# Sparse attention layer: the first eight heads' queries, values and keys made in steps of 512 columns instead of 256, in the order q, v, k

## The chip, the cores and the metric

The kernel runs on one core of one Trainium2 chip. Time is the device time of one execution in microseconds (us). The kernel before took 1060.66 us in the median of three runs (1060.22 to 1060.94). The five engines are TensorE (PE, matmuls; PEld are its weight loads), VectorE (DVE), ScalarE (ACT), GpSimd (POOL) and SyncE (SP), which here only issues DMAs. Each engine works through its own queue in order and waits on semaphores for the others.

## The reference

Four residual layers over a sequence of 512 tokens of width 1024: a gated short convolution, a sparse attention layer, a latent attention layer, and a second convolution. The change concerns the sparse attention layer alone:

```python
q, k, v, z, qi, ki, wi = jnp.split(xn @ w_in, cuts, axis=-1)
q = rope(rmsnorm(q.reshape(bsz, seq, B_HEADS, B_HEAD_DIM), q_norm), positions)
k = rope(rmsnorm(k.reshape(bsz, seq, B_HEADS, B_HEAD_DIM), k_norm), positions)
v = v.reshape(bsz, seq, B_HEADS, B_HEAD_DIM)
...
    rel = jax.nn.relu(jnp.einsum("qhd,sd->qhs", qi_b, ki_b).astype(jnp.float32))
    score = jnp.einsum("qh,qhs->qs", w_b.astype(jnp.float32), rel)
    score = jnp.where(chunk_visible(q_pos, k_pos), score, -jnp.inf)
    top_val, top_idx = lax.top_k(score, topk)
    logits = jnp.einsum("qhd,qkhd->qhk", q_b, k_sel).astype(jnp.float32) * scale
    p = jax.nn.softmax(logits, axis=-1).astype(v_sel.dtype)
    return jnp.einsum("qhk,qkhd->qhd", p, v_sel)
...
return (o * jax.nn.silu(z)) @ w_out
```

There are 16 heads of 64. An indexer of 8 small heads scores all keys for each query, the best 128 are kept, and attention runs over these. The kernel turns the choice into an additive mask and attends densely.

## The kernel before

Activations lie with features on partitions (128) and the 512 tokens along the row. Every large product is made of three matmuls: both operands are split into a high part (`whi`, `xh`) and a low rest (`wlo`, `xl`), and `products` (L279 to L281) adds high by high, high by low and low by high. The weights come by DMA into `raw`; ACT makes `whi` (L155), POOL makes `wlo` (L157), in units of 128 x 512 elements, at most three ahead of PE.

The layer first makes the indexer's projections, then three kinds of work. *Gate steps* (`pz`) multiply 128 columns of z into one bank of 512 tokens. *Query, key and value steps* (`pq`, `pk`, `pv`, function `tokens`) hold tokens on partitions: the activations are the stationary operand and the weight columns stream, 256 at a time for a group of four heads; two blocks of 128 tokens share a bank. *Index scores* (`si`) feed the choice: sixteen rounds of MAX and MATCH_REPLACE on DVE (L801, L802) for each of three query blocks.

After a query or key step, `query_key` copies each bank (ACT, L827), squares it (ACT, L829), sums the squares per head (DVE, L830), rotates (POOL ropea L553, DVE ropeb L557, POOL L560), and works out the norms: sums times a token factor (POOL, L840), mean (L272), a power of -0.5 (L274). For keys POOL also multiplies the tile by the norm (L853). Then `to_features` transposes on PE (L570, tile `tr`), ACT copies out the high part (L573) and DVE subtracts for the low part (L574). Queries are transposed without their norm, which is applied to the scores.

Attention goes through eight pairs of heads. Each pair's scores (`s`, L288) are read by DVE with the mask (L640), made exponentials by ACT (L643), normalised by POOL and ACT (L658, L660), transposed (`pt`, L670) and multiplied with the values (`o`, L691). A `Filler` puts the steps of the later heads between.

In the program, the first eight heads were made as two groups: four gate steps, then q, k, v of heads 0 to 3, two gate steps, q, k, v of heads 4 to 7, all woven with the choice in a ratio of costs (96 to 50). The third and fourth groups are filler during attention. This program order isn't the order on the engines: at build, the framework orders every engine's queue anew by a model of its own (L1184), within what data and buffers allow. Of matter here: eight PSUM banks (tags pj 2, pt 2, o 1, tr 1 and a pair for scores), four `qk` tiles for raw queries and keys, four `whi` and four `wlo` tiles, five `rp` tiles.

Of the kernel before, what the change touches and what calls it, by code (L numbers as in the profile page):

```python
# [17 lines left out]
P = 128  # L18
# [3 lines left out]
NT = S // P  # L22
# [49 lines left out]
def encoder(ctx: ExitStack, tc: tile.TileContext, a, out, depth=4):  # L72
# [20 lines left out]
    def tiny(name, n, dtype=F32, tag="tiny"):  # L93
        return sb.tile([P, n], dtype, name=name, tag=tag, bufs=24)
# [171 lines left out]
    minus_half = const([P, 16], "minus_half")  # L266
    pool.memset(minus_half, -0.5)

    def small_rsqrt(v, n, scale, out=None):

        m = tiny("mean", n)
        pool.tensor_scalar(m, v, scale, EPS, op0=OP.mult, op1=OP.add)  # L272
        y = tiny("y", n) if out is None else out
        pool.tensor_tensor(out=y, in0=m, in1=minus_half[:, :n], op=OP.pow)  # L274
        return y
# [460 lines left out]
    def layer_b(last):  # L736
# [82 lines left out]


        def query_key(group, which, scales, dst, banks):
            raw = []
            sums = tiny("hs", 16)

            def fin(i, b):
                x = tile_of("qk", "qk", (P, 2, 256))
                act_e.activation(x.rearrange("p t c -> p (t c)"), b, AF.Copy)  # L827
                q = tile_of("rp", "qk2", (P, 2, 256))
                act_e.activation(q.rearrange("p t c -> p (t c)"), b, AF.Square)  # L829
                dve.tensor_reduce(sums[:, 8 * i:8 * i + 8], q.rearrange("p t (h d) -> p (t h) d", d=64),  # L830
                                        axis=AX.X, op=OP.add)
                raw.append(x)
                x5, b5 = (y.rearrange("p t (h i j) -> p t h i j", h=4, i=2)
                          for y in (x, b.rearrange("p (t c) -> p t c", c=256)))
                C, T = (tab[:, 2 * i:2 * i + 2] for tab in (tq if which == "q" else tk))
                rotate(x5, x5, C, T, b5)

            yield from tokens(group, act, fin, banks)
            v = tiny("hv", 16)
            pool.tensor_tensor(out=by_head(v), in0=by_head(sums), in1=st["r2"][:, :, None].to_broadcast([P, NT, 4]),  # L840
                               op=OP.mult)
            y = small_rsqrt(v, 16, 1.0 / 64)
            if which == "q":
                pool.tensor_tensor(out=scales, in0=by_head(y), in1=st["rs"][:, :, None].to_broadcast([P, NT, 4]),
                                   op=OP.mult)
            else:
                f = tiny("hf", 16)
                pool.tensor_tensor(out=by_head(f), in0=by_head(y), in1=st["r"][:, :, None].to_broadcast([P, NT, 4]),
                                   op=OP.mult)
            for i, x in enumerate(raw):  # L850
                if which == "k":
                    x3 = x.rearrange("p t (h d) -> p (t h) d", d=64)
                    pool.tensor_tensor(out=x3, in0=x3, in1=f[:, 8 * i:8 * i + 8, None].to_broadcast([P, 8, 64]),  # L853
                                       op=OP.mult)

            for p in range(2):
                to_features(dst[p], lambda t: raw[t // 2][:, t % 2, p * P:(p + 1) * P], P)

        def values(group, dst, banks):
            def fin(i, b):  # L860
                for j in range(2):
                    t = 2 * i + j
                    act_e.activation(dst[i][:, j], b[:, j * 256:(j + 1) * 256], AF.Copy, scale=st["r"][:, t:t + 1])
# [4 lines left out]
        def project(g, tags):  # L868
            s = sets[g] = dict(qs=sb.tile([P, NT, 4], F32, name="qs", tag="qs", bufs=2))
            for n, w in enumerate("qkv"):  # L870
                banks = [bank("p" + w, tags[n % len(tags)]) for _ in range(2)]
                group = a["b_" + w][g]
                if w == "v":
                    s[w] = [tile_of("v", "v", (P, 2, 256)) for _ in range(2)]
                    yield from values(group, s["v"], banks)
                else:
                    s[w] = [[tile_of("T", w + "T", dtype=F32R) for _ in range(2)] for _ in range(2)]
                    yield from query_key(group, w, s["qs"], s[w], banks)

        def job(pair, after, fill):  # L880
            g, i = divmod(pair, 2)

            def scores(outs, t):
# [8 lines left out]
        gate = []  # L892
        token_factors()
# [7 lines left out]
        attention([job(p, p // 2 - 2, ends[p:p + 2]) for p in range(8)],  # L901
                  Filler([project(g, ["pj"]) for g in range(2, 4)] + [gate_steps(a["b_z"][6:], R, gate)]))
# [178 lines left out]
    for i in range(depth):  # L1081
# [3 lines left out]
        elif kind == 1:  # L1085
            enter(a["b_idx"] + a["b_z"][:4])
            for g in range(4):
                enter([a["b_" + w][g] for w in "qkv"])
                if g == 0:
                    enter(a["b_z"][4:6])  # L1090
# [32 lines left out]
def pack(inputs):  # L1123
# [33 lines left out]
    for n, c in (("q", 0), ("k", 1024), ("v", 2048)):  # L1157
        groups["b_" + n] = [put(f"b_{n}_{i}", w, slice(c + 256 * i, c + 256 * i + 256)) for i in range(4)]
# [39 lines left out]
```

## Time and profile before

| | us |
|---|---|
| median of three runs | 1060.66 |
| the profiled execution | 1060.87 |
| its span, first to last instruction | 1059.1 |
| PE busy | 1043.1 |
| POOL busy | 693.9 |
| DVE busy | 525.1 |
| ACT busy | 511.8 |
| first index scores `si` start | 275.5 |
| first query step `pq` starts | 281.4 |
| first attention scores `s` start | 372.0 |

Times in the trace are counted from the span's start. Rows of groups give line, engine, operation, tiles, shape, count, then busy time, mean nanoseconds of one, and the idle time before them. Rows of the timeline give start and length in us. Rows of stretches give, for a window, the busy time and the number of instructions of each engine, the granted PE clock, the DMA share and GB/s. Matmuls overlap in the array, so their rate is read from start to start. The granted clock was 1.000 on average.

### The profile page before, as it was taken

The page shows a single profiled execution, that of the slowest core. Times are in us where ns is not written, and L with a number is a line of the kernel's source. Part 1 is how long each engine was busy: PE and PEld are TensorE (multiplying, and loading weights), DVE is VectorE, ACT ScalarE, POOL GpSimd, SP SyncE. Part 2 cuts the span into 40 slices and gives each one's busy share as a digit, 9 for nine tenths or more (in the row PEclk, how much of TensorE's full clock was granted, in tenths as well). Part 3 has the DMA queues.
Part 4 walks back from the last instruction along what each step waited for, and adds up shares of the span by engine and source line. Part 5 has one row for each costly group of instructions (what it writes and reads, how often), then busy time and mean ns, then how long its engine had stood idle before and what let it go on. Part 6 is the DMA issues. An engine that isn't in the chain of part 4 may idle for free.

```text
span 1059.1 us, 16258 instructions
## 1 busy us (share of the span) xinstructions
PE 1043.1 (98%) x6040; PEld 877.1 (83%) x6040; DVE 525.1 (50%) x1064; ACT 511.8 (48%) x1090; POOL 693.9 (66%) x645
## 2 busy tenths in 40 slices
PE   8999999999999999999999999999999999999998
PEld 6888888899798999998888777687777888888886
DVE  7784333434598984343535234454442654443321
ACT  6243323433444457666745447876764533333231
POOL 6656555666369799686539689788743856555552
PEclk9999999999999999999999999999999999999999
DMA  6333333323222121111223221101211333333332
GB/s 210 103 113 87 97 99 100 90 66 116 80 80 80 61 100 41 61 56 45 58 58 102 75 72 50 41 23 61 61 55 46 100 100 100 100 100 100 100 100 79
DMA packets 27150, 86.43 MB, mean 82 GB/s; under 512 B 3392, under 2 KB 4160, under 8 KB 27072
## 3 DMA queue, kind: packets, MB, share of 16 engines
q1 hardware_dynamic: 26928, 85.36, 26.2%
q8 instruction: 47, 0.77, 0.3%
q14 instruction: 31, 0.25, 0.1%
q10 hardware_dynamic: 144, 0.05, 0.0%
HBM read 83.30 MB, written 2.10 MB: 81 GB/s over the span
## 4 chain that ended last, share of the span: by engine, by line
PE 93%; DVE 3%; ACT 2%; issue 1%; DMA 1%; POOL 0%; SPq 0%; DVEq 0%; ACTq 0%
PE pa L281 10%; PE pa L279 10%; PE pa L280 10%; PE po L279 6%; PE po L281 6%; PE po L280 5%; PE o L691 4%; PE pt L670 3%; PE s L1064 3%; PE pz L279 2%; PE pz L281 2%; PE pz L280 2%; PE s L288 2%; PE tr L570 2%; PE pq L279 2%; PE pk L280 2%
## 5 line engine op out<-in xcount | busy, mean ns | idle before, releaser
L157 POOL TENSOR_TENSOR wlo<-raw,whi 128x512 fp32r<-128x512 f32 (+4 forms) x324 | 410.3, 1274 | 259.2 <-ACT whi L155 248.4
L155 ACT ACTIVATE whi<-raw 128x512 fp32r<-128x512 f32 (+3 forms) x328 | 196.8, 604 | 328.4 <-PE pa L280 159.3
L280 PE MATMUL pa<-xl,whi 128*128 128x512 f32 x512 | 199.5, 390 | 1.0 <-DVE xl L358 1.0
L279 PE MATMUL pa<-xh,whi 128*128 128x512 f32 x512 | 198.5, 390 | 0.9 <-ACT xh L357 0.8
L281 PE MATMUL pa<-xh,wlo 128*128 128x512 f32 x512 | 197.5, 389 | 0.0
L280 PEld LDWEIGHTS pa<-xl,whi 128*128 128x128 f32 x512 | 96.1, 188 | 21.9 <-DVE xl L358 1.9
L279 PEld LDWEIGHTS pa<-xh,whi 128*128 128x128 f32 x512 | 96.0, 188 | 21.3 <-ACT xh L357 1.5
L281 PEld LDWEIGHTS pa<-xh,wlo 128*128 128x128 f32 x512 | 96.1, 188 | 19.9
L658 POOL TENSOR_SCALAR p<-p,rc 128x128 f32<-128x128 f32 (+1 forms) x64 | 69.9, 1099 | 46.2 <-DVE rc L653 41.1
L643 ACT ACTIVATE p<-p,mn 128x128 f32<-128x128 f32 (+3 forms) x128 | 71.0, 557 | 18.2 <-DVE mn L640 18.0
L465 DVE TENSOR_TENSOR cg<-pa,R 128x512 f32<-128x512 f32 x16 | 11.0, 690 | 122.1 <-PE pa L281 119.8
L640 DVE CUSTOM_DVE_ANT_0 p<-s,cmask,qs 128x128 f32<-128x128 f32 (+2 forms) x80 | 37.7, 506 | 39.4 <-PE s L1064 26.7
L279 PE MATMUL pz<-xh,whi 128*128 128x512 f32 x128 | 51.5, 402 | 0.5 <-ACT qk L997 0.5
L281 PE MATMUL pz<-xh,wlo 128*128 128x512 f32 x128 | 50.8, 398 | 0.0
L280 PE MATMUL pz<-xl,whi 128*128 128x512 f32 x128 | 50.4, 394 | 0.0
L280 PE MATMUL po<-xl,whi 128*128 128x512 f32 x128 | 50.1, 391 | 0.0
L675 ACT ACTIVATE p<-pt 128x384 f32<-128x384 f32 (+1 forms) x80 | 38.8, 510 | 23.0 <-PE pt L670 22.6
L280 PE MATMUL po<-glo,whi 128*128 128x512 f32 x128 | 49.8, 389 | 0.0
L279 PE MATMUL po<-xh,whi 128*128 128x512 f32 x128 | 49.5, 400 | 0.0
L279 PE MATMUL po<-ghi,whi 128*128 128x512 f32 x128 | 49.5, 389 | 0.0
L274 POOL TENSOR_TENSOR y<-mean,minus_half 128x16 f32<-128x16 f32 (+1 forms) x18 | 48.8, 2711 | 0.8
L670 PE MATMUL pt<-ident,p 128*128 128x128 f32 x320 | 47.9, 277 | 0.6 <-ACT p L675 0.6
(244 smaller groups left out, 2423.5 us busy)
## 6 DMA issues: line engine op xcount, KB each, us to landing
raw<-in_a_in SPq DMA_DIRECT2D x63, 512.0 KB, 3.9
raw<-in_a_out SPq DMA_DIRECT2D x16, 512.0 KB, 3.9
raw<-in_b_z SPq DMA_DIRECT2D x8, 512.0 KB, 3.5
raw<-in_b_q SPq DMA_DIRECT2D x8, 512.0 KB, 3.4
raw<-in_b_k SPq DMA_DIRECT2D x8, 512.0 KB, 3.5
raw<-in_b_v SPq DMA_DIRECT2D x8, 512.0 KB, 3.5
raw<-in_c_z SPq DMA_DIRECT2D x8, 512.0 KB, 3.5
raw<-in_b_out SPq DMA_DIRECT2D x8, 384.0 KB, 3.2
```

The lines of the kernel that those rows point to most:

```text
L155: act_e.activation(hi[:, :, :n], raw[:, j:j + m], AF.Copy)
L157: e.tensor_tensor(out=lo, in0=raw[:, j:j + m, :n - few], in1=hi[:, :, :n - few].bitcast(F32), op=OP.subtract)
L274: pool.tensor_tensor(out=y, in0=m, in1=minus_half[:, :n], op=OP.pow)
L279: nc.tensor.matmul(o, l[0], r[0], start=first, stop=False)
L280: nc.tensor.matmul(o, l[0], r[1], start=False, stop=False)
L281: nc.tensor.matmul(o, l[1], r[0], start=False, stop=last)
L640: dve.tensor_tensor_reduce(out=p[:, w], in0=banks[e][:, w], in1=j["masks"](t), scale=j["qs"](e, t), scalar=-GONE, op0=OP.add, op1=OP.min, ...
L643: act_e.activation(p[:, w], p[:, w], AF.Exp, bias=mn[e][:, i:i + 1], scale=-1.0, accum_out=sm[:, e * n + i:e * n + i + 1])
L658: pool.tensor_scalar(p[:, w], p[:, w], rc[:, i:i + 1], None, op0=OP.mult)
L670: pe.transpose(b[:, i:i + P], p[:, i:i + P], ident)
L675: act_e.activation(p[:, :n], b[:, :n], AF.Copy)
L691: pe.matmul(o[64 * e:64 * e + 64, t * P:(t + 1) * P], j["v"](e, kb), x[e][:, i:i + P], start=first, stop=t == 0)
```

## The change

Heads 0 to 7 are made as one group: the weight matrices of q, k and v are cut into one block of 512 columns and two of 256. A step of 512 columns takes four banks (pj, pj, pt, pt), one for each block of 128 tokens. The order is three gate steps, q, gate step 4, v, gate step 5, k, gate step 6; the latter three gate steps use bank o, and transposes from there on use bank tr alone. Four steps of the choice are issued before the weave. `query_key` and `values` take any width: the sums of squares lie in one tile of 32 columns, worked on in place, and the power runs once for eight heads. Each raw tile holds one block of 128 tokens by 512 columns, as large as before. Heads 8 to 15 keep their steps of 256 columns. Weights enter in the new order.

```diff
     def tiny(name, n, dtype=F32, tag="tiny"):
-        return sb.tile([P, n], dtype, name=name, tag=tag, bufs=24)
+        return sb.tile([P, n], dtype, name=name, tag=tag, bufs=20)
...
     def small_rsqrt(v, n, scale, out=None):
-        m = tiny("mean", n)
+        m = tiny("mean", n) if out is not v else v
...
         def query_key(group, which, scales, dst, banks):
+            heads = group.n // 64
+            per = NT // len(banks)
             raw = []
-            sums = tiny("hs", 16)
+            sums = sb.tile([P, NT * heads], F32, name="hs", tag=f"hs{heads}", bufs=2)
 
             def fin(i, b):
-                x = tile_of("qk", "qk", (P, 2, 256))
+                x = tile_of("qk", "qk", (P, per, group.n))
...
             yield from tokens(group, act, fin, banks)
-            v = tiny("hv", 16)
-            pool.tensor_tensor(out=by_head(v), in0=by_head(sums), in1=st["r2"][:, :, None].to_broadcast([P, NT, 4]),
-                               op=OP.mult)
-            y = small_rsqrt(v, 16, 1.0 / 64)
+            y = by_token(sums, heads)
+            pool.tensor_tensor(out=y, in0=y, in1=st["r2"][:, :, None].to_broadcast([P, NT, heads]), op=OP.mult)
+            small_rsqrt(sums, NT * heads, 1.0 / 64, sums)
             if which == "q":
-                pool.tensor_tensor(out=scales, in0=by_head(y), in1=st["rs"][:, :, None].to_broadcast([P, NT, 4]),
-                                   op=OP.mult)
+                for g, x in enumerate(scales):
+                    pool.tensor_tensor(out=x, in0=y[:, :, 4 * g:4 * g + 4],
+                                       in1=st["rs"][:, :, None].to_broadcast([P, NT, 4]), op=OP.mult)
             else:
-                f = tiny("hf", 16)
-                pool.tensor_tensor(out=by_head(f), in0=by_head(y), in1=st["r"][:, :, None].to_broadcast([P, NT, 4]),
-                                   op=OP.mult)
+                pool.tensor_tensor(out=y, in0=y, in1=st["r"][:, :, None].to_broadcast([P, NT, heads]), op=OP.mult)
...
-            for p in range(2):
-                to_features(dst[p], lambda t: raw[t // 2][:, t % 2, p * P:(p + 1) * P], P)
+            for p, x in enumerate(dst):
+                to_features(x, lambda t: raw[t // per][:, t % per, p * P:(p + 1) * P], P)
...
+        def project(which, gs, banks):
+            group = a["b_" + which][0 if len(gs) > 1 else gs[0] - 1]
...
+        def late(g):
+            new_set(g)
+            for which in "qkv":
+                yield from project(which, [g], lambda: [bank("p" + which, "pj") for _ in range(2)])
...
-        early = chain(gate_steps(a["b_z"][:4], R, gate, "pj"), project(0, ["pj", "pt"]),
-                      gate_steps(a["b_z"][4:6], R, gate, "pj"), project(1, ["pj", "pt"]))
+        def four(name):
+            return lambda: [bank(name, tag) for tag in ("pj", "pj", "pt", "pt")]
+
+        early = chain(gate_steps(a["b_z"][:3], R, gate, "pj"), only_tr(),
+                      *(x for i, which in enumerate("qvk") for x in
+                        (project(which, [0, 1], four("p" + which)), gate_steps(a["b_z"][3 + i:4 + i], R, gate, "o"))))
         for _ in range(3):
             next(early)
         turn_index()
-        run(weave((early, 96), (select(), 50)))
+        chosen = select()
+        for _ in range(4):
+            next(chosen)
+        run(weave((early, 96), (chosen, 46)))
...
-            enter(a["b_idx"] + a["b_z"][:4])
-            for g in range(4):
+            enter(a["b_idx"] + a["b_z"][:3])
+            for i, w in enumerate("qvk"):
+                enter([a["b_" + w][0], a["b_z"][3 + i]])
+            for g in range(1, 3):
                 enter([a["b_" + w][g] for w in "qkv"])
...
-        groups["b_" + n] = [put(f"b_{n}_{i}", w, slice(c + 256 * i, c + 256 * i + 256)) for i in range(4)]
+        groups["b_" + n] = [put(f"b_{n}_{i}", w, slice(c + d, c + e))
+                            for i, (d, e) in enumerate(((0, 512), (512, 768), (768, 1024)))]
```

More of the change, by code (lines that the diff above doesn't have):

```diff
@@ L818, in token_factors, with by_token @@
                     pool.tensor_scalar(st[name], st["r"], k, 0.0, op0=OP.mult, op1=OP.add)
+        def by_token(x, heads):
+            return x.rearrange("p (t h) -> p t h", h=heads)
         def query_key(group, which, scales, dst, banks):
+            heads = group.n // 64
+            per = NT // len(banks)
             raw = []
[L823 removed]
+            sums = sb.tile([P, NT * heads], F32, name="hs", tag=f"hs{heads}", bufs=2)
             def fin(i, b):
[L826 removed]
+                x = tile_of("qk", "qk", (P, per, group.n))
                 act_e.activation(x.rearrange("p t c -> p (t c)"), b, AF.Copy)
[L828 removed]
+                q = tile_of("rp", "qk2", (P, per, group.n))
                 act_e.activation(q.rearrange("p t c -> p (t c)"), b, AF.Square)
@@ L859, in values @@
         def values(group, dst, banks):
+            per = NT // len(banks)
             def fin(i, b):
-                for j in range(2):
-                    t = 2 * i + j
-                    act_e.activation(dst[i][:, j], b[:, j * 256:(j + 1) * 256], AF.Copy, scale=st["r"][:, t:t + 1])
+                for j in range(per):
+                    t = per * i + j
+                    for g in range(len(dst) // 2):
+                        c = j * group.n + g * 256
+                        act_e.activation(dst[2 * g + t // 2][:, t % 2], b[:, c:c + 256], AF.Copy,
+                                         scale=st["r"][:, t:t + 1])
@@ L864, in values, with new_set @@
             yield from tokens(group, act, fin, banks)
         sets = {}
[L868 to L878, printed above, removed]
+        def new_set(g):
+            sets[g] = dict(qs=sb.tile([P, NT, 4], F32, name="qs", tag="qs", bufs=2))
@@ new lines, in project @@
+        def project(which, gs, banks):
+            group = a["b_" + which][0 if len(gs) > 1 else gs[0] - 1]
+            if which == "v":
+                dst = []
+                for g in gs:
+                    sets[g]["v"] = [tile_of("v", "v", (P, 2, 256)) for _ in range(2)]
+                    dst += sets[g]["v"]
+                yield from values(group, dst, banks())
+            else:
+                dst = []
+                for g in gs:
+                    sets[g][which] = [[tile_of("T", which + "T", dtype=F32R) for _ in range(2)] for _ in range(2)]
+                    dst += sets[g][which]
+                yield from query_key(group, which, [sets[g]["qs"] for g in gs], dst, banks())
@@ L892, in layer_b, with only_tr @@
         gate = []
+        def only_tr():
+            early_turns[0] = False
+            yield from ()
         token_factors()
-        early = chain(gate_steps(a["b_z"][:4], R, gate, "pj"), project(0, ["pj", "pt"]),
-                      gate_steps(a["b_z"][4:6], R, gate, "pj"), project(1, ["pj", "pt"]))
+        for g in range(2):
+            new_set(g)
+        def four(name):
[3 more added lines that the diff above has]
+                        (project(which, [0, 1], four("p" + which)), gate_steps(a["b_z"][3 + i:4 + i], R, gate, "o"))))
         for _ in range(3):
@@ L898, in layer_b @@
         turn_index()
-        run(weave((early, 96), (select(), 50)))
+        chosen = select()
+        for _ in range(4):
+            next(chosen)
+        run(weave((early, 96), (chosen, 46)))
         ends = [0, 11, 22, 34, 45, 56, 68, 73, 78]
         attention([job(p, p // 2 - 2, ends[p:p + 2]) for p in range(8)],
-                  Filler([project(g, ["pj"]) for g in range(2, 4)] + [gate_steps(a["b_z"][6:], R, gate)]))
+                  Filler([late(g) for g in range(2, 4)] + [gate_steps(a["b_z"][6:], R, gate)]))
         branch_out(a["b_out"], gate, last)
```

12 lines of the change are left out of this document (5 added, 7 removed).

## The prediction

> **What bounds the kernel now.** I read the page's busy shares first, then busy time by stretches around the place of the change, then the list of waits.
>
> ```profile
> span 1059.1 us, 16258 instructions
> PE 1043.1 (98%) x6040; PEld 877.1 (83%) x6040; DVE 525.1 (50%) x1064; ACT 511.8 (48%) x1090; POOL 693.9 (66%) x645
> ...
> core 0: us, PE busy (x) PEld busy (x) DVE busy (x) ACT busy (x) POOL busy (x), PEclk, DMA share, GB/s
> 254.00:281.00 27.00, 25.20 (x120) 19.67 (x119) 21.11 (x52) 10.23 (x21) 15.77 (x17) 1.00 0.33 107
> 281.00:372.00 91.00, 91.00 (x701) 84.23 (x699) 78.37 (x181) 41.15 (x80) 66.09 (x55) 1.00 0.22 71
> 372.00:400.00 28.00, 27.60 (x228) 25.77 (x227) 22.00 (x56) 17.29 (x42) 27.66 (x26) 1.00 0.27 92
> ...
> PE pk L279 <- ACT qk L829: 0.4, 1, 0.4
> ```
>
> TensorE (PE) is busy for 1043.1 of 1059.1 us. From 281 us, where the first query step runs, to 372 us, where the first attention scores start, it never pauses; in the next 28 us its one pause is 0.4 us. So PE is the bound here: time is won only by less PE work, and every pause that the change brings is lost in full, as nothing later has idle time to give back. POOL is nearly full after 372 us (27.66 of 28 us).
>
> **The bigger steps.** 256 columns now, 512 afterwards.
>
> ```profile
> L279 PE MATMUL pq<-whi,xh 128*128 128x256 f32 x128 | 37.0, 291 | 0.0
> ...
> 269.66 0.39 PE L279 MATMUL pz<-xh,whi 128*128 128x512 f32 x1
> ...
> 275.14 0.39 PE L279 MATMUL pz<-xh,whi 128*128 128x512 f32 x1
> ...
> 287.36 0.28 PE L280 MATMUL pq<-wlo,xh 128*128 128x256 f32 x1
> ...
> 290.22 0.28 PE L280 MATMUL pq<-wlo,xh 128*128 128x256 f32 x1
> ```
>
> Durations overlap in the array, so the price is the distance from start to start. Between the first pair of rows lie 24 steps of 512 columns: 5.48/24 = 0.228 us. Between the second lie 24 of 256: 2.86/24 = 0.119 us. One wide matmul for two narrow ones saves 0.238 - 0.228 = 0.010 us. Sixteen heads take nine such groups of 128 matmuls (three products for each of q, k, v), so the first eight take 576; 288 remain: 288 x 0.010 = **-2.9 us**. The columns streamed are the same, which is why halving the count saves so little.
>
> **The order.** What is moved is dearer. The order on PE at the first attention scores (s), before; pv is the value step of the second four heads:
>
> ```order
> L281 MATMUL pv<-whi,xl 128x256
> L279 MATMUL pv<-whi,xh 128x256 x2
> L288 MATMUL s<-kT,qT 128x128 x2
> L280 MATMUL pv<-wlo,xh 128x256
> L281 MATMUL pv<-whi,xl 128x256
> ```
>
> The scores stand inside other heads' matmuls. Now; pq and pk at the two ends are the third group's steps, tr the transposes of the eight heads' keys (one row per pair of heads), pt those of the probabilities:
>
> ```order
> L281 MATMUL pq<-whi,xl 128x256
> L570 MATMUL tr<-ident,qk 128x128 x4
> L288 MATMUL s<-kT,qT 128x128 x2
> L570 MATMUL tr<-ident,qk 128x128 x4
> L288 MATMUL s<-kT,qT 128x128 x4
> L288 MATMUL s<-kT,qT 128x256 x6
> L570 MATMUL tr<-ident,qk 128x128 x4
> L288 MATMUL s<-kT,qT 128x384 x6
> L570 MATMUL tr<-ident,qk 128x128 x4
> L670 MATMUL pt<-ident,p 128x128 x6
> L288 MATMUL s<-kT,qT 128x512 x6
> L279 MATMUL pk<-whi,xh 128x256
> ```
>
> All keys of eight heads are now made last, and attention begins with them. Between the last key matmul and the first key transpose PE has 24 gate matmuls and 96 of pq: 24 x 0.228 + 96 x 0.119 = 16.9 us. PE takes its queue in order, so what stands behind a late transpose waits too.
>
> What the transposes wait for is POOL. Before, at the first four heads' keys:
>
> ```order
> L840 TENSOR_TENSOR hv<-hs,br_2322 128x16
> L272 TENSOR_SCALAR mean<-hv 128x16
> L274 TENSOR_TENSOR y<-mean,minus_half 128x16
> L157 TENSOR_TENSOR wlo<-raw,whi 128x512
> L848 TENSOR_TENSOR hf<-y,rtok 128x16
> L157 TENSOR_TENSOR wlo<-raw,whi 128x512
> L853 TENSOR_TENSOR qk<-qk,hf 128x512 x2
> ```
>
> Now, at the eight heads' keys (L846 to L857 are the same operations, renumbered):
>
> ```order
> L553 TENSOR_TENSOR ropea<-qk,table 128x512
> L157 TENSOR_TENSOR wlo<-raw,whi 128x512
> L846 TENSOR_TENSOR hs<-hs,br_2322 128x32
> L560 TENSOR_TENSOR qk<-ropea,ropeb 128x512
> L157 TENSOR_TENSOR wlo<-raw,whi 128x512
> L560 TENSOR_TENSOR qk<-ropea,ropeb 128x512
> L272 TENSOR_SCALAR hs<-hs 128x32
> L157 TENSOR_TENSOR wlo<-raw,whi 128x512 x2
> L274 TENSOR_TENSOR hs<-hs,minus_half 128x32
> L157 TENSOR_TENSOR wlo<-raw,whi 128x512
> L853 TENSOR_TENSOR hs<-hs,rtok 128x32
> L857 TENSOR_TENSOR qk<-qk,hs 128x512 x4
> ```
>
> Everything is doubled; ahead of these rows stand three more L553, two more L560 and two more L157. In all: four L553, four L560, seven L157, four L857, the power L274 and three small ones, before the last key tile is fit to transpose. Their prices:
>
> ```profile
> 359.83 2.55 POOL L157 TENSOR_TENSOR wlo<-raw,whi 128x512 fp32r<-128x512 f32 x2
> 363.33 0.22 POOL L840 TENSOR_TENSOR hv<-hs,br 128x16 f32<-128x16 f32 x1 [0.95 <-DVE hs L830]
> ...
> 366.80 2.56 POOL L553 TENSOR_TENSOR ropea<-qk,table 128x512 f32<-128x512 f32 x2
> ...
> 372.00 1.29 POOL L560 TENSOR_TENSOR qk<-ropea,ropeb 128x512 f32<-128x512 f32 x1
> ...
> 385.91 2.06 POOL L853 TENSOR_TENSOR qk<-qk,hf 128x512 f32<-128x512 f32 x2
> ...
> L274 POOL TENSOR_TENSOR y<-mean,minus_half 128x16 f32<-128x16 f32 x16 | 46.8, 2923 | 0.7
> L274 POOL TENSOR_TENSOR rtok<-mean,minus_half 128x4 f32<-128x4 f32 x2 | 2.1, 1039 | 0.2
> ```
>
> The power at 32 columns is not in the trace. Four columns take 1.04 us and sixteen 2.92, so 0.157 us a column, and 32 would be 5.4 us; if it did not grow, 2.9. I take the line through both. Sum: 4 x 1.28 + 4 x 1.29 + 7 x 1.28 + 5.4 + 3 x 0.22 + 4 x 1.03 = 29.4 us. POOL can start about 1 us before PE's last key matmul: the first of four banks ends 3 x 3 x 0.228 = 2.1 us earlier and is copied by ACT. So the last key tile is ready 28.4 us after it; PE runs dry at 16.9 and can do three early transposes (0.4 us): a pause of **+11.1 us**. Low end: no growth of the power, 1 us less for overlapping rows, gives 7.6; high end: L853's slow pair (2.96 us, below) and waits for DVE, 15. The first set before shows that such a chain is long, and what hid it:
>
> ```profile
> 310.95 0.60 ACT L827 ACTIVATE qk<-pk 128x512 f32<-128x512 f32 x1
> ...
> 337.68 2.96 POOL L853 TENSOR_TENSOR qk<-qk,hf 128x512 f32<-128x512 f32 x2
> ...
> 341.48 0.60 PE L570 MATMUL tr<-ident,qk 128*128 128x128 f32 x4
> ```
>
> Half as much work took from 310.95 to 340.6 us, and PE did the value, gate and query steps of others meanwhile.
>
> **Thin work after it.** The four transpose rows share the one bank tr; each must be copied by ACT, then subtracted by DVE, before the next. The third group's pk must wait too: its two banks are pq's, and pq's copies need key tiles' buffers (four, all held until transposed).
>
> ```profile
> L573 ACT ACTIVATE kT<-tr x8: 576/598/656, 342.8 to 497.1; 128x512 fp32r<-128x512 f32 x8
> L574 DVE TENSOR_TENSOR kT<-tr,kT x8: 677/686/692, 345.8 to 497.8; 128x512 fp32r<-128x512 f32 x8
> ...
> 375.12 0.77 PE s L288 x10
> 381.84 0.72 PE s L288 x6
> 387.39 0.89 PE s L288 x6
> ...
> 405.90 1.02 PE pt L670 x8
> ```
>
> Each round is 0.60 + 0.60 + 0.69 = 1.9 us, four 7.6; DVE's reading of the first scores stands between, about 3 us, so pk starts some 10.6 us after the last key tile. PE's own work in that time is 4 x 0.6 + 0.9 + 0.7 + 0.9 + 0.8 = 5.7 us. Idle: 5, and 1 for the next round's transposes of pq: **+6 us** (low 2, all of DVE hidden; high 10).
>
> **The clock.** A pause of 11 us is new to this kernel. The nearest row is its end, where PE has nothing to do:
>
> ```profile
> 1050.00:1055.30 5.30, 5.22 (x24) 3.98 (x22) 0.55 (x2) 0.00 (x0) 0.00 (x0) 1.00 0.13 49
> 1055.30:1059.10 3.80, 0.00 (x0) 0.00 (x0) 0.65 (x1) 0.00 (x0) 0.00 (x0) 0.95 0.18 69
> ```
>
> The granted clock (0.95) falls within 3.8 us of idleness. How far it falls and how fast it returns no row tells. Low end 0 (back at once); high end: the 5.7 us and the next 33 narrow matmuls (3.9 us) twice as long on the path, 9. Much of the thin work waits for other engines anyway, so I take **+3 us**. The Trainium skill, "TensorE: Matmul & The Clock Gate", section "What's actually happening", says that about 3.4 us of idleness halves the clock and about 3.4 us of steady work restores it. By that rule this term would be some 4 to 5 us and the sum 1079.5; without it 1075.
>
> The remaining edits cost nothing that shows: the value copies are as many and as large; fewer small POOL operations for queries save under 1 us on an engine that PE does not wait for there; the tiny pool's 20 buffers serve fewer tiles; weights, bytes and splits are the same.
>
> **Sum.** -2.9 + 11.1 + 6 + 3 = +17.2 us. The profiled execution took 1060.87 us (median of the runs 1060.66): 1060.87 + 17.2 = **1078 us**.
>
> **Rivals.** *The clock costs nothing*: the first matmul brings it back. 1075 us. For it: the thin work is limited by hand-overs; against it: the 0.95. *The keys come later still*: DVE finishes the index mask ahead of the key subtractions in its queue.
>
> ```profile
> 358.36 0.68 DVE L801 MAX8 m<-score 128x8 f32<-128x512 f32 x1
> ...
> 359.86 0.69 DVE L801 MAX8 m<-score 128x8 f32<-128x512 f32 x1
> ```
>
> A round costs 1.5 us; eleven stand behind the first key bank, with the key's own reductions about 24 us, so DVE is done 5 us before POOL. If it lags 10 us, the loss grows by 5: 1083. *Faster*: POOL ends its key rows within PE's 16.9 us of cover and the transposes find their data; then only the wide steps count, 1060.87 - 2.9 = 1058 us. It decides at 16.9 + 1 = 18 us of POOL time; even the low end of my sum (26) is far above.
>
> **Numbers.** Forecast 0.55, clock free 0.25, later keys 0.13, faster 0.04, a mix that cancels 0.03. Range: the low ends of both pauses with the clock free give 1060.87 - 2.9 + 7.6 + 2 = 1067.6, unlikely together, so it starts at 1069; it ends at 1084, with later keys. Differences of 0.2% (2.1 us) can be told here. Faster 0.04, same 0.02, slower 0.94.
>
> **What would show it.** Busy PE in the stretch after the last pk of the wide step: a hole of 8 to 15 us that ends on POOL's L857, then one of the thin kind, with tr waiting on DVE kT; a granted clock under 1.00 there. The wide pq, pk, pv must stand 0.228 us apart. Wrong if PE's list of waits names no POOL at L570, or if L274 at 32 columns is near 3 us and the chain ends before PE runs dry.

## The result and the profile after

The changed kernel took **1075.31 us** in the median of four runs (1075.05 to 1076.00), the kernel before beside it 1060.77 us: a ratio of 1.014, with a 95% interval from 1.0128 to 1.0152, or 14.5 us more. The forecast was 1078, in a range from 1069 to 1084.

The profiled execution of the changed kernel took 1075.19 us. First from its page: the span, the busy time, and the clock that TensorE was granted in 40 slices of the span.

```profile
span 1073.4 us, 15663 instructions
PE 1046.8 (98%) x5752; PEld 864.4 (81%) x5752; DVE 525.7 (49%) x1064; ACT 512.4 (48%) x1090; POOL 691.8 (64%) x638
PEclk9999999999999969999999999999999999999999
```

There are 288 matmuls fewer (5752 against 6040) and yet 3.7 us more of busy PE, and one slice has a clock of 0.6. Busy time by stretches around that slice, in the columns that the prediction showed:

```profile
363.00:381.00 18.00, 18.00 (x121) 16.64 (x120) 17.20 (x39) 9.01 (x16) 17.30 (x16) 1.00 0.28 89
381.00:395.00 14.00, 3.31 (x16) 1.93 (x15) 6.14 (x13) 0.68 (x2) 13.31 (x9) 0.65 0.24 75
395.00:406.00 11.00, 9.72 (x44) 6.54 (x45) 6.87 (x21) 7.66 (x22) 4.08 (x5) 0.51 0.00 0
406.00:412.00 6.00, 5.98 (x55) 5.51 (x54) 3.51 (x10) 4.78 (x11) 5.83 (x6) 1.00 0.01 4
```

Up to 381 us PE is full. In the next 14 us it works for 3.31 while POOL works for 13.31: the hole. From 395 to 406 PE looks busy, but at a clock of 0.51. The list of PE's waits in that stretch (total, times, longest) names who ended the hole, and the POOL timeline (start, duration) shows the key chain from its first to its last instruction:

```profile
PE tr L570 <- POOL qk L857: 10.6, 4, 9.0
PE s L288 <- ACT kT L573: 0.7, 1, 0.7
PE s L288 <- DVE mn L640: 0.4, 1, 0.4
PE tr L570 <- DVE kT L574: 0.2, 1, 0.2
```

```profile
364.79 2.56 POOL L553 TENSOR_TENSOR ropea<-qk,table 128x512 f32<-128x512 f32 x2
...
383.40 5.44 POOL L274 TENSOR_TENSOR hs<-hs,minus_half 128x32 f32<-128x32 f32 x1
...
390.35 4.04 POOL L857 TENSOR_TENSOR qk<-qk,hs 128x512 f32<-128x512 f32 x4
```

From 364.79 to 394.39 the chain lasts 29.6 us. On PE's timeline the first key transpose waits for it, and the work behind it is slow:

```profile
391.44 0.48 PE L570 MATMUL tr<-ident,qk 128*128 128x128 f32 x1 [9.04 <-POOL qk L857]
...
396.33 1.11 PE L570 MATMUL tr<-ident,qk 128*128 128x128 f32 x4 [0.25 <-DVE kT L574]
...
404.11 1.65 PE L288 MATMUL s<-kT,qT 64*128 64x512 f32 x6
```

Four transposes take 1.11 us and six wide scores 1.65 us; before they took 0.60 and 0.89. Slices of 1 us place the clock's fall and its return:

```profile
385.00:386.00 1.00, 0.00 (x0) 0.00 (x0) 0.96 (x2) 0.00 (x0) 1.00 (x1) 0.63 0.13 49
386.00:387.00 1.00, 0.00 (x0) 0.00 (x0) 0.93 (x4) 0.00 (x0) 1.00 (x1) 0.50 0.00 0
...
404.00:405.00 1.00, 1.00 (x5) 0.79 (x6) 1.00 (x3) 1.00 (x4) 1.00 (x2) 0.50 0.00 0
405.00:406.00 1.00, 1.00 (x6) 0.35 (x5) 0.77 (x3) 1.00 (x4) 1.00 (x2) 0.63 0.00 0
```

A mean of 0.63 is full speed for 0.26 us and half for 0.74: the clock halves at 385.3 us and is back at 405.7, 20 us later.

### The profile page after: what moved, and what is told of

It is laid out like the page before. It is cut to its first block, busy times and chain, and to the rows that moved or that the text cites. A ratio compares the mean times of both kernels' runs of the same rounds, so it can differ in the third digit from the quotient of the medians.

```text
span 1073.4 us, 15663 instructions
## 1 busy us (share of the span) xinstructions
PE 1046.8 (98%) x5752; PEld 864.4 (81%) x5752; DVE 525.7 (49%) x1064; ACT 512.4 (48%) x1090; POOL 691.8 (64%) x638
## 4 chain that ended last, share of the span: by engine, by line
PE 91%; DVE 3%; POOL 2%; ACT 1%; issue 1%; DMA 1%; SPq 0%; DVEq 0%
PE pa L281 10%; PE pa L279 10%; PE pa L280 10%; PE po L279 5%; PE po L281 5%; PE po L280 5%; PE o L691 4%; PE pt L670 3%; PE s L1101 3%; PE pz L279 2%; PE pz L281 2%; PE pz L280 2%; PE s L288 2%; PE tr L570 2%; PE pv L281 1%; PE pk L281 1%
## 5 line engine op out<-in xcount | busy, mean ns | idle before, releaser
L155 ACT ACTIVATE whi<-raw 128x512 fp32r<-128x512 f32 (+3 forms) x328 | 196.8, 604 | 333.4 <-PE pa L280 159.3
L675 ACT ACTIVATE p<-pt 128x384 f32<-128x384 f32 (+1 forms) x80 | 38.7, 509 | 20.0 <-PE pt L670 18.4
L281 PE MATMUL po<-xh,wlo 128*128 128x512 f32 x128 | 47.9, 395 | 0.0
```

The lines of the kernel that those rows point to most:

```text
L155: act_e.activation(hi[:, :, :n], raw[:, j:j + m], AF.Copy)
L281: nc.tensor.matmul(o, l[1], r[0], start=False, stop=last)
L675: act_e.activation(p[:, :n], b[:, :n], AF.Copy)
```

## The experiments

Twelve kernels were run, in four sets of four, four, two and two, each set with its own runs of the kernel before. In the table, "ratio" is to these. Beside the runs the kernel before took 1060.13 to 1060.45 us, beside the changed kernel 1060.77, so a difference of two medians from different sets is uncertain by some 0.6 us.

| run | what | us | ratio (95%) |
|---|---|---|---|
| 1 | order q, k, v | 1068.5 | 1.0071 (1.0057 to 1.0085) |
| 2 | matmuls that fill the hole | 1073.2 | 1.0118 (1.0101 to 1.0134) |
| 3 | power of the keys left out | 1069.8 | 1.0085 (1.0071 to 1.0099) |
| 4 | six key tile buffers | 1075.1 | 1.0134 (1.0120 to 1.0148) |
| 5 | key norm on DVE | 1074.6 | 1.0134 (1.0116 to 1.0152) |
| 6 | key norm and product on DVE | 1073.4 | 1.0115 (1.0099 to 1.0131) |
| 7 | q, k, v and key norm on DVE | 1070.8 | 1.0091 (1.0077 to 1.0106) |
| 8 | q, k, v and four short powers | 1069.0 | 1.0078 (1.0064 to 1.0091) |
| 9 | keys in two sets, values last | 1066.0 | 1.0051 (1.0035 to 1.0066) |
| 10 | weight splits off POOL | 1071.2 | 1.0098 (1.0082 to 1.0115) |
| 11 | order of the change, width undone | 1065.8 | 1.0050 (1.0036 to 1.0063) |
| 12 | keys in two sets around the values | 1070.4 | 1.0096 (1.0081 to 1.0111) |

**Run 3: the chain's length.** The theory: the pause is the part of POOL's chain that is longer than PE's cover. A multiplication stands in for the power, so the eight heads' keys are not normalised.

```diff
-            small_rsqrt(sums, NT * heads, 1.0 / 64, sums)
+            if which == "k" and heads == 8:
+                pool.tensor_tensor(out=sums, in0=sums, in1=minus_half, op=OP.mult)
+            else:
+                small_rsqrt(sums, NT * heads, 1.0 / 64, sums)
```

> The changed kernel without the power for the keys of the first eight heads: a multiplication of the same 32 columns stands in its place on POOL (about 0.25 us instead of 5.44), so those keys are not normalised. Theory (POOL's chain sets the end of the pause): the pause of 10.6 us becomes 5.4, the clock still falls, time 1070 (1069 to 1071). Rival (DVE, whose mask ends at 387.4 us, or another engine stands right behind POOL): the pause shrinks by less than 3, time above 1072.

Measured 1069.84 us. The wait on POOL, from the list of PE's waits:

```profile
PE tr L570 <- POOL qk L860: 5.4, 4, 3.3
```

The power took 5.4 us and the multiplication takes 0.26. The wait is 5.2 us shorter and the profiled span 5.4 (1068.0 against 1073.4). POOL's chain is what PE waits for, and the wait follows its length.

**Run 2: the clock and the thin work apart.** 44 matmuls of 512 columns whose result nobody uses are put behind the last key step, to fill the hole.

```diff
+            if which == "k" and heads == 8:
+                d = bank("fill", "o")
+                z = act(0)[0]
+                for _ in range(44):
+                    pe.matmul(d, z[:, :P], z, start=True, stop=True)
```

> The changed kernel with 44 more matmuls of 512 columns (44 x 0.228 = 10.0 us) on PE behind the last key step, into bank o, read by nobody; nothing else is touched. They fill the 10.6 us in which PE waited for the keys, so PE never rests and the clock should stay at 1.00. Theory A (the halved clock is dear in the thin stretch): the stretch from the first scores to pk shrinks from 11.3 us by 4 to 6, time 1069 to 1071. Theory B (the thin stretch waits for other engines and the clock costs next to nothing): time 1074 to 1075.

Measured 1073.16 us, between the two. On PE the 44 matmuls stand right behind the last key matmul, from 365.65 to 375.6 us; the gate and query matmuls are pushed back into the stretch where the hole was. Busy time by stretches: that stretch, the thin work behind it, and the last 3.41 us of the thin work.

```profile
381.00:393.00 12.00, 12.00 (x92) 11.54 (x90) 7.46 (x13) 3.47 (x6) 11.75 (x11) 1.00 0.14 44
393.00:403.00 10.00, 6.16 (x46) 3.96 (x45) 6.20 (x20) 7.69 (x21) 5.66 (x6) 1.00 0.34 107
399.26:402.67 3.41, 1.92 (x12) 1.11 (x12) 2.53 (x8) 3.24 (x9) 3.17 (x4) 1.00 0.00 0
```

In this execution the clock stays at 1.00, and the thin work has 10.00 - 6.16 = 3.8 us of idle time. So at full clock the thin stretch costs 3.8 us by itself. What the half clock adds to it shows between the last transpose of the first pair's keys and the third group's first key matmul, in the changed kernel and then in run 2:

```profile
394.44 0.48 PE L570 MATMUL tr<-ident,qk 128*128 128x128 f32 x1 [0.52 <-POOL qk L857]
...
405.69 0.39 PE L279 MATMUL pk<-whi,xh 128*128 128x256 f32 x1
```

```profile
392.78 0.27 PE L570 MATMUL tr<-ident,qk 128*128 128x128 f32 x1
...
402.73 0.36 PE L279 MATMUL pk<-whi,xh 128*128 128x256 f32 x1 [0.64 <-DVE ropeb L557]
```

That is 11.25 us against 9.95, so 1.3 us is the net price of the half clock there: at half speed PE's own work fills idle time that it would have had anyway. The profiled span is 1070.4 us, 3.0 us under that of the changed kernel, but the other 1.7 us are not the clock's. PE ran out of work at 382.41 us in the changed kernel, 12.0 us before that last transpose; the filling work lasts only 44 x 0.228 = 10.0 us, and in run 2 the first pair's transposes run among the query matmuls without a wait (POOL's chain, with fewer weight splits in it, lasted from 365.15 to 390.17 us, 25.0 us). Nor do all executions agree: two of the four had a mean clock of 1.000 and took 1072.20 (the profiled one) and 1071.27 us, two had 0.995 and took 1075.03 and 1074.12, 2.8 us more in the mean. No trace of the latter two shows where their clock fell, so 1.3 us rests on one pair of traces; the price may be up to about 3 us.

**Run 4: give PE other work.** Six tile buffers instead of four, so that the third group's key steps can run inside the hole. (The index keys' tiles share another pool, and the probabilities have nine buffers instead of ten.)

```diff
-    "p": 10, "qk": 4,
+    "p": 9, "qk": 6,
-        key = [sb.tile([P, P], F32, name="key", tag="key", bufs=4) for _ in range(NT)]
+        key = [tile_of("gate", "key", (P, P)) for _ in range(NT)]
```

> The changed kernel with six buffers instead of four for raw queries and keys; to make room the index keys lie in gate tiles and the probabilities have nine buffers instead of ten. The order stays q, v, k. On PE the 96 matmuls of the third group's key step (11.5 us) then stand ahead of the key transposes, because its query step can be copied out without waiting for the key tiles. Theory (the pause is long only since four key tiles hold all four buffers): the pause falls from 10.6 to under 1 us, the clock stays at 1.00, the thin stretch costs about 5: time 1060 (1058 to 1063). Rival (POOL is then loaded with those weights' low parts and the keys come later by as much): time above 1068.

Measured 1075.14 us: nothing won. From the list of PE's waits, and the POOL timeline:

```profile
PE tr L570 <- POOL qk L857: 6.3, 4, 4.7
PE pk L279 <- ACT qk L835: 1.9, 1, 1.9
```

```profile
388.69 2.55 POOL L553 TENSOR_TENSOR ropea<-qk,table 128x512 f32<-128x512 f32 x2
391.20 1.48 POOL L157 TENSOR_TENSOR wlo<-raw,whi 128x512 fp32r<-128x512 f32 x1
...
399.58 4.05 POOL L857 TENSOR_TENSOR qk<-qk,hs 128x512 f32<-128x512 f32 x4
```

PE does get its key steps (it is busy for 12.07 of the 14 us from 381), so the buffers were what held them back. But that work needs POOL too: the queries' rotations and more weight splits now stand in the queue ahead of the keys' product, which ends at 403.6 us, 9.2 us later than in the changed kernel. Cover that uses the late engine lengthens what it covers. Some 4 us were also lost later (149.91 of 154 us busy between 430 and 584 us), 2.5 us of them on DVE's reading of scores (mn) and 1.6 us on ACT's copies of the transposed probabilities (p, L675); whether the ninth buffer or the shifted order makes them was not tried.

**Run 1: keys before values.** Then 22 us of value steps would cover the chain.

```diff
-                      *(x for i, which in enumerate("qvk") for x in
+                      *(x for i, which in enumerate("qkv") for x in
```

> One edit to the changed kernel: the order q, k, v instead of q, v, k (weights enter in that order too). Steps of 512 columns, four banks, one bank for transposes and index scores ahead all stay. Theory (the keys coming last is the whole loss): the value step's 96 matmuls (21.9 us) now cover the keys' POOL work of 29.6 us together with the last gate step; no wait of tr on POOL L857 above 1 us, clock 1.00 throughout, and what is left is the gain of the wide steps: 1060.7 - 3 = 1058 us (1057 to 1060). Rival (the wide steps themselves cost: four banks at once, eight heads' POOL work in one lump): the time stays above 1068.

Measured 1068.49 us: the long wait at the transposes is gone, and 8 us are lost all the same. PE's waits between 250 and 600 us, the POOL timeline, and slices of busy time:

```profile
PE pv L280 <- POOL wlo L157: 5.2, 1, 5.2
PE pv L279 <- DVE ropeb L557: 2.0, 2, 1.7
```

```profile
356.36 5.44 POOL L274 TENSOR_TENSOR hs<-hs,minus_half 128x32 f32<-128x32 f32 x1
361.77 5.10 POOL L157 TENSOR_TENSOR wlo<-raw,whi 128x512 fp32r<-128x512 f32 x4
```

```profile
361.00:363.00 2.00, 0.00 (x0) 0.00 (x0) 2.00 (x6) 0.00 (x0) 2.00 (x3) 0.61 0.02 4
363.00:368.00 5.00, 4.91 (x12) 3.85 (x13) 4.79 (x11) 0.63 (x1) 4.41 (x6) 0.50 0.34 112
```

The value steps need their weights split by POOL (wlo), and these splits now stand behind the keys' power. The same queue hurts from its other side: 7.2 us of waiting and about 2.5 us of half clock, less 2.9 us for the wide steps, make 6.8 of the 7.5 us by which its profiled span (1066.6) exceeds that of before.

**Runs 5, 6 and 7: take the norm off POOL.** The keys' small operations (two products, the mean, an inverse root by three Newton steps) go to DVE; in run 6 the product over the four tiles too; run 7 is run 1 with the norm on DVE.

```diff
+            e = dve if which == "k" and heads == 8 else pool
-            pool.tensor_tensor(out=y, in0=y, in1=st["r2"]...
-            small_rsqrt(sums, NT * heads, 1.0 / 64, sums)
+            e.tensor_tensor(out=y, in0=y, in1=st["r2"]...
+            dve.tensor_scalar(sums, sums, 1.0 / 64, EPS, op0=OP.mult, op1=OP.add)
+            rsqrt(sums, ..., sums)
```

> The change as it is, with the key norm's thirteen small operations (two products, the mean, and the inverse root by Newton steps in place of the power) on VectorE and not on GpSimd; the final product over the tiles stays on GpSimd. A (the pause is the length of GpSimd's queue, and the power is 5.4 us of it): the pause on GpSimd falls from 10.6 to about 5 us, as in the run with a multiply in the power's place, whose time was 1069.8: 1069.5 (1068.5 to 1070.5). B (VectorE, in order behind the index selection, gives the norm late, so the pause only changes its owner): above 1073.

> As the run before it, and the final product over the four key tiles goes to VectorE too: of GpSimd's chain only the rotation and the weight splits are left, which in the changed kernel's trace end at about 380.5, 2 us before TensorE runs out of work. A: the pause falls from 10.6 us to 1 to 4 us, TensorE stays at its full clock, and of the thin work behind it 2 to 3 us of idle are left as in the run with the filling matmuls: 1063 (1060 to 1066). B (VectorE's queue, with the selection in it, is the next bound: the products wait behind the selection's steps until about 390): 1068 or more.

> Order queries, keys, values (the run that gave 1068.5), with the key norm's small operations on VectorE. In that run TensorE stood 5.2 us in the value steps, waiting for the low part of a weight block that stood behind the 5.4 us power in GpSimd's queue, and ran for some 5 us at half clock afterwards. A (the power in the queue in front of the weight splits is the cost): that wait goes, and with it about 2.5 us at half clock: 1060.5 (1059 to 1062.5). B (the waits come from VectorE, busy 22.9 of 23 us there, which now gets 1.4 us more): 1066 or more.

Measured 1074.64, 1073.40 and 1070.80 us: the first forecast was wrong in all three, and the rival's right. DVE's timeline in run 5, and POOL's product there:

```profile
376.23 1.27 DVE L849 TENSOR_SCALAR hs<-hs 128x32 f32<-128x32 f32 x1
...
381.79 0.72 DVE L260 TENSOR_TENSOR w<-u,hs 128x32 f32<-128x32 f32 x1
...
386.00 0.17 DVE L260 TENSOR_TENSOR w<-u,hs 128x32 f32<-128x32 f32 x1
```

```profile
390.00 4.04 POOL L862 TENSOR_TENSOR qk<-qk,hs 128x512 f32<-128x512 f32 x4 [4.64 <-DVE hs L858]
```

Two things made 16 us (373.75 to 389.9) out of fourteen operations, of which the last six take 0.17 or 0.18 us each. Between any two of them the order on DVE has a step of the index selection (0.7 us). And the first eight, while POOL is busy, take 0.65 to 1.27 us each; from 385.4 us, when POOL's queue had run dry, the same L260 takes 0.17. The selection's own steps (MAX8) take 0.69 us in both cases. The Trainium skill, "SBUF — State Buffer", section "Who interferes with whom", says that a DVE instruction with two SBUF inputs contends with a GpSimd instruction that reads SBUF, and that one in a two-port mode and a GpSimd instruction block each other for a whole instruction. The durations here agree: none is longer than a GpSimd operation (1.28 us). POOL's work went down and the keys came no sooner: the product starts at 390.00, against 390.35 in the changed kernel. In run 6 PE's wait of 8.1 us ends on DVE's product. In run 7 the wait for wlo is gone, as expected, and 3.5 us on the keys' product and 2.0 us on a high weight part (ACT, L155) are new.

**Run 8: one long power or four short ones.** Run 1 with the norm tile by tile.

```diff
+                for i, x in enumerate(raw):
+                    c = sums[:, 8 * i:8 * i + 8]
+                    ...
+                    pool.tensor_tensor(out=c, in0=c, in1=minus_half[:, :8], op=OP.pow)
+                    ...
+                    pool.tensor_tensor(out=x3, in0=x3, in1=c[:, :, None].to_broadcast([P, 8, 64]), op=OP.mult)
```

> Order queries, keys, values, everything on GpSimd as in the change, but the key norm is taken tile by tile: four powers of 8 columns (about 1.65 us each by the line through 4, 16 and 32 columns) with weight splits let in between them, in place of one power of 32 columns; GpSimd has about 2.5 us more work in all. A (what hurts is one long operation ahead of a weight split, not the sum of GpSimd's work): the 5.2 us wait shrinks to 0 to 1.5 us, 1062 (1060 to 1064). B (the sum of GpSimd's work sets it): 1068 or more.

Measured 1068.95 us. PE's waits between 340 and 400 us:

```profile
PE pv L280 <- POOL wlo L157: 2.5, 1, 2.5
PE tr L570 <- POOL qk L854: 2.3, 1, 2.3
```

Each power of 8 columns took 1.63 to 1.67 us, as the line through 4 and 16 columns says. The wait for the weights halves, and a transpose that stood in time in run 1 now waits 2.3 us: the sum is nearly the same (4.8 against 5.2 us). That speaks for the sum of POOL's work in these 20 us and not for the longest operation. It is not shown cleanly, as the pieces also gave POOL more to do (2.5 us by the estimate above), and waits on DVE's ropeb rose from 2.2 to 3.2 us.

**Run 10: take the weight splits out of the queue instead.** In the order of the change, the low parts of the last early gate group and of the third group's queries and keys are made on DVE.

```diff
+    split_on_dve = [a["b_z"][5], a["b_q"][1], a["b_k"][1]]
-        e = dve if count[0] < 4 else pool
+        e = dve if count[0] < 4 or g in split_on_dve else pool
```

> The change as it is, with the low parts of the weight blocks that stand in the key chain's queue (last early gate group, third group's queries and keys) made on VectorE, not on GpSimd. GpSimd's chain for the keys then holds nothing but the keys: 29.6 - 7 x 1.28 = 20.6 us. A (the order of one queue that serves both the keys and the weights is what makes the pause): the pause falls from 10.6 us to 2 to 5 us, TensorE's clock stays up for most of the thin work behind it: 1066 (1063 to 1069). B (VectorE's small and medium operations stretch to the length of GpSimd's, as in the two runs with the norm on VectorE, where 128 x 32 operations took 0.65 to 1.27 us while GpSimd was busy and 0.17 us when it was idle; rotations and splits on VectorE then come late instead): 1071 or more.

The wait came out as expected, the time did not: 1071.16 us. The wait, and slices of busy time:

```profile
PE tr L571 <- POOL qk L858: 3.8, 4, 1.7
```

```profile
385.00:388.00 3.00, 1.40 (x3) 0.55 (x3) 2.86 (x7) 0.00 (x0) 2.50 (x3) 0.55 0.50 175
388.00:395.00 7.00, 4.35 (x23) 3.12 (x24) 6.53 (x20) 3.15 (x10) 0.00 (x0) 0.50 0.00 0
395.00:402.00 7.00, 6.72 (x28) 4.40 (x29) 6.98 (x20) 5.59 (x15) 5.26 (x5) 0.50 0.00 0
402.00:404.00 2.00, 2.00 (x17) 2.00 (x17) 1.38 (x5) 1.88 (x4) 2.00 (x4) 0.91 0.03 8
```

The pause is 6.8 us shorter and the time only 4.2 us: no single wait is longer than 1.7 us, but the waits before the transposes leave PE busy for only 0.9 us of the 3.4 us before 385.3, where the clock halves, and the gaps in the thin work keep it there until 402.4. What is won on the pause is in part lost again to idle time in the thin work (1.5 us on mn: DVE, which now also splits weights, ends the selection at 398.2 us, against 387.4 in the changed kernel, and reads the scores between its steps).

**Run 11: width or order?** The order of the change in steps of 256 columns, two sets of four heads after one another.

```diff
-                      *(x for i, which in enumerate("qvk") for x in
-                        (project(which, [0, 1], four("p" + which)), gate_steps(a["b_z"][3 + i:4 + i], R, gate, "o"))))
+                      project("q", [0], ...), project("q", [1], ...), gate_steps(a["b_z"][3:4], R, gate, "o"),
+                      project("v", [0], ...), project("v", [1], ...), gate_steps(a["b_z"][4:5], R, gate, "o"),
+                      project("k", [0], ...), project("k", [1], ...), gate_steps(a["b_z"][5:6], R, gate, "o"))
```

> The order of the change (queries, gate, values, gate, keys, gate) with its width undone: each step is taken for two sets of four heads in turn, 256 columns each. A (the loss is that one chain serves eight heads; with two chains of half the length the first starts 11.4 us earlier, the first two pairs' keys are there when their scores are due, and key steps of the third group fill TensorE until the other two come): a pause of 0 to 3 us, and the 2.9 us of the wide steps are not won: 1062 (1060 to 1064). B (the order alone, keys after the values, makes the loss, since GpSimd has the same total to do after the last key step): 1070 or more.

Measured 1065.78 us, between the two bounds. Slices of busy time, and PE's longest wait there:

```profile
384.70:388.11 3.41, 1.75 (x16) 1.24 (x16) 2.55 (x6) 2.10 (x5) 3.41 (x3) 1.00 0.42 154
388.00:390.00 2.00, 0.51 (x2) 0.54 (x3) 2.00 (x8) 1.72 (x5) 2.00 (x2) 0.53 0.00 0
391.52:394.94 3.42, 3.42 (x18) 3.42 (x17) 1.21 (x7) 1.81 (x6) 3.42 (x6) 0.50 0.06 20
```

```profile
PE pk L279 <- ACT qk L835: 1.8, 1, 1.8
```

The order, with all that came with it but the width (the banks, the four early steps of the choice, the ratio of the weave), costs 5.6 us, with no wait over 1.8 us: 4.1 us of waits in small pieces, and up to 2.7 us because the clock was halved from 388.1 to 394.9 us with PE busy. The wide steps, with their chain for eight heads, cost another 9 us (14.5 - 5.6), although they save PE 2.9 us of work.

**Runs 9 and 12: keep the wide queries and values, halve the keys.** Run 9: queries, gate, keys, gate, keys, gate, values. Run 12: queries, gate, keys, values, gate, keys, gate.

```diff
+                      project("q", [0, 1], four("pq")), gate_steps(a["b_z"][3:4], R, gate, "o"),
+                      project("k", [0], ...), gate_steps(a["b_z"][4:5], R, gate, "o"),
+                      project("k", [1], ...), gate_steps(a["b_z"][5:6], R, gate, "o"),
+                      project("v", [0, 1], four("pv")))
```

> Queries and values of eight heads in steps of 512 columns as in the change, but the keys again in two sets of four heads and 256 columns, each with a gate group behind it, and the values last: queries, gate, keys, gate, keys, gate, values. A (the loss is the long key chain of eight heads at once, with the 32-column power and four tiles; a chain of half the length hides behind 5.5 us of gate steps and 22 us of value steps): no pause of TensorE above 2 us between 281 and 412 us, and of the wide steps two thirds of 2.9 us are left as gain: 1058 (1056.5 to 1060). B (any order with wide steps collides with the index selection on VectorE there, as the runs with queries, keys, values did): 1063 or more.

> Queries and values of eight heads in steps of 512 columns, keys in two sets of four heads: queries, gate, first keys, values, gate, second keys, gate. The first two pairs' scores can run while GpSimd works on the second set. By rows: that chain is two rotations, two sums, a power of 2.9 us, two products and 0.7 us of small ones (10.8 us) with some six splits of 1.28 us and 2.3 us of probabilities, 20.8 us; TensorE has 5.5 us of gate, 11.4 us of queries and some 3.5 us of scores and transposes as cover, 20.4 us. A (only the eight-head chain at the end costs): no pause over 2 us from 281 to 412 us, 1058.5 (1057 to 1060.5). B (wide steps ahead of or among the index selection cost some us by themselves, as in the run with keys in halves and the values last, whose time was 1066): 1063 or more.

Measured 1065.99 and 1070.36 us; 1058 and 1058.5 were expected. In run 9 no wait is over 1.7 us, as expected, but those between 281 and 430 us add up to 5.5 us, and the mean clock is 0.84 from 395 to 406 us. The waits alone are too many: two executions with a mean clock of 1.000 took 1064.49 and 1064.93 us. In run 12 the loss lies much earlier. Its waits from 300 to 345 us, and its stretch from 325 to 340 us:

```profile
PE pv L279 <- DVE ropeb L557: 4.4, 1, 4.4
PE tr L570 <- DVE qT L574: 3.2, 2, 1.9
```

```profile
325.00:340.00 15.00, 8.68 (x41) 6.20 (x42) 14.83 (x35) 6.31 (x12) 5.55 (x6) 0.84 0.18 61
```

The end, from 340 us on, was cured (70.89 of 72 us busy). But four banks of values follow the keys at once, and must wait until DVE, busy for 14.83 of 15 us with the selection, has read the keys out of two of them. No version with wide steps came under the kernel before.

## Why the prediction was right, and where it was off

- **The wide steps, -2.9 us**: held. Between a query matmul at 280.77 us (280.78 in run 11) and the last key matmul, 265 of the 288 wide matmuls run, without a wait. The changed kernel is 1.7 us quicker there than run 11, though six more index scores and four more transposes, about 1.1 us (ten such rows took from 281.91 to 282.99 us), stand in that stretch: 2.8 us. The last key matmuls of the two kernels, from their timelines:

```profile
365.07 0.39 PE L281 MATMUL pk<-whi,xl 128*128 128x512 f32 x1
```

```profile
366.81 0.28 PE L281 MATMUL pk<-whi,xl 128*128 128x256 f32 x1
```

- **The pause, +11.1 us**: PE waited 10.6 us for POOL. Reckoned as the prediction did, from PE's running dry (382.41 us) to the last key tile (394.39) less 0.4 us of transposes, it is 11.6. The chain was 29.6 us long (29.4 predicted) and began 0.3 us ahead of the last key matmul (1 predicted); PE ran dry 17.3 us after that matmul (16.9 predicted). The power at 32 columns, the one price that no row showed, took 5.44 us (5.4 by the line through two points; it would have been 2.9 had it not grown). Run 3 shows that the pause follows the chain one for one. That key tiles' buffers hold the third group's key steps back held too (run 4).
- **The thin work, +6 us**: this term was too large. At full clock it costs 3.8 us (run 2). The step that failed is the one that set 3 us for DVE's reading of the first scores between the hand-overs, and 1 us for the next round's transposes. In run 2 PE waits 0.7 us for that reading (mn), 1.6 us at the hand-overs of the keys (kT) and for none of the next round's transposes; 1.5 us go to two waits that the prediction did not name (0.9 for probabilities from POOL, 0.6 for ropeb).
- **The clock, +3 us**: too large as well, by the traces: 1.3 us net (run 2), though the executions of run 2 leave room for up to about 3. The sum with the measured terms is -2.8 + 11.6 + 3.8 + 1.3 = +13.9 us; the profiled executions differ by 1075.19 - 1060.87 = 14.3. In the changed kernel itself the last two terms cannot be told apart: its thin work shows only some 1.3 us of waits, because PE, at half speed, works through what would be idle time. The prediction added the two; their split rests on run 2, which has the one without the other. So the mechanism was right, and 1078 was too high by these two terms: together they were 3.9 us too large, and the pause was 0.5 too small.
- The Trainium skill's "TensorE: Matmul & The Clock Gate", section "What's actually happening" (about 3.4 us of idleness halve the clock, about 3.4 us of steady work restore it), is borne out as to the half: the granted clock went to 0.50 some 2.9 us after the last matmul, sooner than 3.4. It came back 5.4 us after PE's last gap, and what that depends on is in the last section. The price that the prediction drew from that rule, 4 to 5 us, was further off than the 3.
- **Rivals**: "the clock costs nothing" fell, as the first matmul did not bring it back (0.50 for 20 us). Its time of 1075 was nevertheless the nearest: its argument, that hand-overs limit the thin work, holds in the main, and the rest is luck, since it had the same too large term for the thin work. "Later keys" fell: DVE ended the mask at 387.4 us, 7 us before POOL's last key tile. "Faster" fell by the 29.6 us chain.

What stays open is whether an order exists in which the wide steps pay. In the changed kernel and in the ten versions that were meant to mend it, POOL, DVE or a bank was late by some us, and in the profiled execution of each the clock fell as well. That the old order is the best possible has not been shown.

## What to carry to other kernels

When a bottleneck engine is full, fusing two of its steps into one saves little (here 0.010 us a matmul), while the engines that finish each step get their work in blocks of twice the length; price the longest such block, and all that shares its queue, against the work that covers it. Cover that needs the late engine itself is no cover (run 4), and work moved to another engine has to be priced in that engine's queue, between its other work, and at the longer times that it takes there beside a busy GpSimd (run 5). A pause or a thin stretch that leaves TensorE busy for less than half of 3.4 us can halve its clock; here that added 1.3 us by the traces to a pause of 11.6, as the work behind it waited for other engines anyway.

## What the runs showed of the hardware

- The power on GpSimd is linear in the columns: 1.04 us at 4, 1.66 at 8, 2.92 at 16 and 5.44 at 32 columns of 128 partitions, 0.157 us a column.
- VectorE's 128 x 32 operations on SBUF take 0.17 or 0.18 us beside an idle GpSimd and 0.65 to 1.27 us beside a busy one (run 5); MAX8 takes 0.69 us either way.
- The granted clock halved 2.9 us after PE's last matmul in the changed kernel and 3.6 us in run 1. Inside an execution its half-clock stretches last 3.41 us (as in run 9), 6.83 (runs 1, 11 and 12), 13.65 (runs 3 and 4), 17.07 (runs 5, 6 and 10) or 20.48 us (the changed kernel): all are multiples of 3.41. So it changed only at the ends of windows of 3.41 us, and these windows can be counted from any fall.
- It came back at the end of the first such window in which PE had no gap at all, in all 17 returns of these traces (402.32 to 405.74 us in the changed kernel, 391.52 to 394.94 in run 11). Stretches of 3.6 us without a gap that lie across two windows, which the changed kernel and run 3 have before that, did not bring it back; from the last gap it took 5.4 us in the changed kernel, 5.2 in run 1, 6.0 in run 3, 5.0 in run 10 and 5.4 in run 11.
- It fell at the end of a window with little busy PE, also where PE was never idle for long: in run 11 at 388.1 us, after a window with 1.75 us of busy time and no gap over 1.1 us before it. In all 14 traces, between 12 and 1055 us, it always fell after a window with 1.4 us of busy PE or less (0.57 in the changed kernel, 0.89 in run 10) and never after one with 1.96 or more (in run 2 the thin windows had 2.45, 2.08 and 1.92 us and kept 1.00). In between both happened: the same 1.75 us kept it in run 1 (340.95 to 344.36 us). What decides there the traces do not show.
